# Layer 1's bias rows on their way through DRAM: one small store and a DRAM-to-DRAM copy in place of a store of 128 copies

## The chip, the cores and the metric

One Trainium2 chip, one of its cores in use. Times are device microseconds (us) of one execution of the whole program; lower is better.

## The reference: what is computed

Two decoder layers on 256 tokens of width 1024, all in float32. Layer 0 mixes tokens by a gated delta rule (8 heads), layer 1 by sparse attention (8 heads in 2 groups: compressed, selected and window branches). Both layers attend to 256 memory tokens with 4 heads, multiply by an output projection and end in a gated channel mixer.

```python
for i in range(DEPTH):                       # 2 layers
    h = rms_norm(x, norm_mix_w[i])
    mem_n = rms_norm(mem, mem_norm_w[i])
    proj = h @ w_in[i]                       # heads of the mixer, and queries for the memory
    mix = gdn_mixer(...) if i == 0 else nsa_mixer(..., rel_bias, ...)
    mo = memory_attention(qm, mem_n, mem_w_kv[i])
    x = x + concatenate([mix, mo], -1) @ w_out[i]
    x = x + conv_glu(rms_norm(x, norm_ffn_w[i]), ...)
return rms_norm(x, final_norm_w)
# in nsa_mixer, to the scores of each query t and key p:
#   bias = rel_bias[t5_bucket(t - p), head]   (32 buckets x 8 heads)
```

The change is about that last bias alone. It depends on the distance t - p only, so a head has 384 different values over the distances of two 128-token halves (some masked).

## The kernel before, in words

**How the work runs.** The program is recorded as tile operations; a list scheduler (`Sched`, with cost estimates of its own) fixes an order for each engine before the program is built, and each engine then runs its own list strictly in that order. All DMAs are issued from one list, that of SP. An SP entry whose semaphores are not up holds back all entries behind it. Every operation is issued at one line, L379 (`Op.run`), so the profile's line numbers don't tell operations apart; tile names do.

**Weights.** `Weights.prep` loads 8 blocks of 128x128 (512 KB) into a tile `wr`, ScalarE (ACT) casts it to `wh`, VectorE (DVE) subtracts to get `wl`; TensorE (PE) then does three matmuls per block (`pj<-xh,wh`, `xl,wh`, `xh,wl`). There are three buffers each of `wr`, `wh` and `wl`. For the memory's keys and values the same is done with 256 KB tiles `mr`, `mh`, `ml` and PSUM tiles `pf`.

**The place of the change** is the seam between the last memory attention of layer 0 and its output projection `w_out` (12 weight tiles of 8 blocks each). By priority the scheduler has pulled two things forward into this seam: layer 1's memory keys and values (`mr`, `pf`, `vm`) and layer 1's bias tables. The bias tables are made so: a 33x8 by 33x384 matmul gives the 384 values of each head on 8 partitions, ACT copies them to `bb` (8 partitions x 384), and one DMA writes `bb` 128 times over to the DRAM tile `sk` (8 x 128 x 384, 1.5 MB). For each head a DMA then reads `sk` with a row step of 383 in place of 384, so that partition p gets the row shifted by p: the tile `bias` (128 x 2 x 128).

```python
sk = sc.tile("sk", [H, P, HOTN], F32, "sk", 1)                       # L1171
SY.dma_start(sk, bb[:, None, :].to_broadcast([H, P, HOTN]))          # L1172
for h in range(H):                                                   # L1173
    bt = K("bias", H, shape=(P, 2, P))
    SY.dma_start(bt, sk.raw(... ap=[[HOTN - 1, P], [P, 2], [1, P]]))
```

The eight `bias` tiles are read some 280 us later, by the attention of layer 1.

Of the kernel before, what the change touches and what calls it, by code (L numbers as in the profile page):

```python
# [10 lines left out]
F32 = mybir.dt.float32  # L11
# [8 lines left out]
P = 128  # L20
# [5 lines left out]
H = 8  # L26
# [25 lines left out]
HOTN = 384  # L52
# [1 line left out]


class Sched:
    """Records tile operations, orders them with a list scheduler over the engines, then issues them."""

    ENG = ("tensor", "vector", "scalar", "gpsimd", "sync")
    LAT = {"tensor": 0.27, "vector": 0.17, "scalar": 0.2, "gpsimd": 0.18, "sync": 0.13}  # L60
# [188 lines left out]
        return out  # L249

    def sooner(self, op, e, eng_t, ready):
        """Whether engine e would finish op before the other engine that can run it."""
        f = {}
        for x, c in op.alt.items():
            t = max(eng_t[x], op.rt)
            wait = sum((o.alt[x] * 0.5 if o.alt else o.cost) for o in ready[x] if o.prio < op.prio and o.rt <= t)
            f[x] = t + wait + c
        return f[e] <= min(f.values())
# [39 lines left out]


class Sub(Vt):  # L300
    """A part of a whole-kernel tile that has its own dependences."""

    def __init__(self, base, fn, shape, tag):
        super().__init__(base.cls, shape, base.dt, tag, 1)
# [201 lines left out]
def body(ctx, tc, xT, memT, vecs, consts, rows, relb, w_few, w_in0, w_out0, w_up0, w_dn0, w_in1, w_out1, w_up1, w_dn1,  # L506
         w_mem0, w_mem1, cw1, cw2, out):
    nc = tc.nc
    pools = {}
# [9 lines left out]
    classes = dict(CLASSES)  # L519
    sc = Sched(nc, classes)  # L520
    PE, V, A, PO, SY = (sc.t[e] for e in Sched.ENG)
# [8 lines left out]
    def K(tag, bufs=2, dt=F32, shape=(P, S)):  # L530
        return sc.tile("k", shape, dt, tag, bufs)

    def Dd(tag, bufs=2, shape=(P, 512), dt=F32):
        return sc.tile("d", shape, dt, tag, bufs)

    def Sm(tag, shape, bufs=2):
        return sc.tile("s", shape, F32, tag, bufs)

    def pj(tag="pj"):
        if tag != "pj":  # L540
            return sc.tile("ps", [P, S], F32, tag, 4)
        return sc.tile("ps", [P, S], F32, "pj", 4)
# [10 lines left out]
    def mm(*a, **kw):  # L553
        PE.matmul(*a, **kw)
# [11 lines left out]
        return ps  # L566

    def proj_t(ws, b0, xs, tag="pj"):
        """Token-major products: [128 tokens, 256 columns] for both halves of the sequence."""
        ps = [pj(tag), pj(tag)]  # L570
        n = len(xs)
        for k in range(n):
            wh, wl = ws.block(b0 + 2 * k, 2)
            xh, xl = xs[k]
            for t in range(2):
                c = slice(t * P, (t + 1) * P)
                with PE.group():
                    mm(ps[t], xh[:, c], wh, start=k == 0, stop=False)
                    mm(ps[t], xh[:, c], wl, start=False, stop=False)
                    mm(ps[t], xl[:, c], wh, start=False, stop=k == n - 1)  # L580
        return ps

    def proj_few(hl, xs, n):
        """Few columns: both parts of the weights are one stationary operand of 2n columns."""
        ps = pj()
        for k in range(KD):
            xh, xl = xs[k]
            with PE.group():
                mm(ps[:2 * n], hl[:, k], xh, start=k == 0, stop=False)
                mm(ps[:2 * n], hl[:, k], xl, start=False, stop=k == KD - 1)  # L590
        return ps[:2 * n]
# [15 lines left out]
    x = [Sub(xall, lambda r, k=k: r[:, k], [P, S], f"x{k}") for k in range(KD)]  # L607
# [61 lines left out]
    def evac(ps, rs, dst):  # L669
        V.tensor_tensor(out=dst, in0=ps, in1=rs, op=OP.mult)  # L670

# [1 line left out]
    kTm, vm = {}, {}  # L673
    def mem_load(k):
        mt = Dd("mt", 4)
# [58 lines left out]
            mm(po[:, :S], vm[layer, h // 2, m2][:, (h % 2) * P:(h % 2 + 1) * P], pT[:, m2 * S:(m2 + 1) * S], start=m2 == 0, stop=m2 == 1)  # L734
        return hilo(po[:, :S], "mix", 12)

# [1 line left out]
    def ffn(layer, w_up, w_dn, rs, xs):  # L738
        wu = Weights(sc, w_up, 2 * KF * KD, "w", 3)
        wd = Weights(sc, w_dn, KD * KF, "w", 3)  # L740
# [32 lines left out]
    def normed(col, keep="row"):  # L773
        hs, acc = [], None
        for k in range(KD):
            hs.append(split(x[k], col + k, "x", KD))
            acc = sq_acc(acc, x[k])
        r = rstd_fin(acc, keep=keep)
        return (hs,) + (r if keep == "col" else (r,))

    # ================= layer 0 =================
    def x_load(k):
        SY.dma_start(xall[:, k:k + 2], xT[:, k * S:(k + 2) * S].rearrange("p (k t) -> p k t", k=2), also_out=x[k:k + 2])

# [38 lines left out]
        hs.append((hi, lo))  # L823
    mix = [None] * 12

    # decay and write strength, token-major [128, tile, head]
    ps = proj_few(wba, hs, 16)
    ba = K("ba", 1, shape=(32, S))
    A.copy(ba, ps)
# [71 lines left out]
    US = NB * (IB * P + IB)  # L901

    def silu(dst, y, src, fast):
        """silu(y), or twice that from the table that Exp is in."""
        if fast:
            A.activation(dst, src, AF.Silu)
            return
        th = K("ct")
        A.activation(th, src, AF.Tanh, scale=0.5)
        V.scalar_tensor_tensor(dst, th, 1.0, y, op0=OP.add, op1=OP.mult)  # L910
# [24 lines left out]
    def gdn_pair(p):  # L935
# [53 lines left out]
                V.scalar_tensor_tensor(AT[e][:, t], pgm[:, t * S + P:(t + 1) * S], rr[:, t:t + 1], g1[:, t], op0=OP.mult, op1=OP.mult)  # L989

        yield
        # inverses of the 16 x 16 diagonal blocks, one block on each partition
        sl = sc.tile("scl", [4 * US], F32, "scl", 2)
        for e in range(2):
            SY.dma_start(sl.raw(lambda r, e=e: bass.AP(tensor=r.tensor, offset=r.offset + 2 * e * US,
                                                      ap=[[P, P], [US, 2], [1, P]]), [P, 2, P]), LL[e])
        Lb = K("Lb", 1, shape=(4 * NB, IB, IB))
        SY.dma_start(Lb, sl.raw(lambda r: bass.AP(tensor=r.tensor, offset=r.offset,
                                                 ap=[[IB * P + IB, 4 * NB], [P, IB], [1, IB]]), [4 * NB, IB, IB]))
# [4 lines left out]
        for k in range(IB - 1):  # L1004
# [8 lines left out]
                                             ap=[[IB * IB, 4 * NB], [4 * NB * IB * IB, 2], [1, IB * IB]]),  # L1013
# [9 lines left out]
                EV.tensor_tensor(out=DX[e][:, w].rearrange("p u (c i) -> p u c i", c=NB),  # L1023
                                         in0=cd[:, w, 2 * e:2 * e + 2][:, :, None, :].to_broadcast([P, 2, NB, IB]), in1=bd, op=OP.mult)

        # doubling of the diagonal blocks: 16 to 32 over whole chunks, then by blocks of 32 and of 64
        for e in range(2):
            lm = K("lm", 4, shape=(P, 2, P))
            EV.tensor_tensor(out=lm, in0=LL[e], in1=cst[:, C_LVL - C_TRI:C_LVL - C_TRI + P][:, None, :].to_broadcast([P, 2, P]),
                             op=OP.mult)  # L1030
# [7 lines left out]
            with PE.group():  # L1038
                for t in range(2):
# [3 lines left out]
                                                      ap=[list(r.ap[0]), [S + IB, 2], [2 * IB, NB], [1, IB]]), [P, 2, NB, IB])  # L1043
# [25 lines left out]
                            V.tensor_tensor(out=DX[e][O, 0, :, E], in0=DX[e][O, 0, :, E], in1=two(p2[O, :2 * n]), op=OP.subtract)  # L1069

        yield
        # chunk recurrence and outputs
        zs = {}
        for e, h in enumerate(hd):
            ps = proj(w0, (h * 4 + 3) * KD, hs)
# [2 lines left out]
        for e, h in enumerate(hd):  # L1078
# [38 lines left out]
            y = K("oz", 1)  # L1117
# [32 lines left out]
    hs, rs = normed(V_NFFN)  # L1150
    ffn(0, w_up0, w_dn0, rs, hs)

    # ================= layer 1 =================
    hs, rs, rc = normed(V_NMIX + KD, "col")
    rcs = Sm("rcs", [P, 2], 1)
    V.tensor_scalar(rcs, rc, SCALE, None, op0=OP.mult)

    # relative-position bias tiles
    rbe = Sm("rbe", [33, H], 1)
    V.memset(rbe, NEG)  # L1160
    SY.dma_start(rbe[:32], relb)
# [2 lines left out]
    bias = []  # L1164
# [3 lines left out]
    mm(pb[:H, :HOTN], rbe, hot, start=True, stop=True)  # L1168
    bb = Dd("bb", 1, (H, HOTN))
    A.copy(bb, pb[:H, :HOTN])  # L1170
    sk = sc.tile("sk", [H, P, HOTN], F32, "sk", 1)  # L1171
    SY.dma_start(sk, bb[:, None, :].to_broadcast([H, P, HOTN]))  # L1172
    for h in range(H):  # L1173
        bt = K("bias", H, shape=(P, 2, P))
        SY.dma_start(bt, sk.raw(lambda r, h=h: bass.AP(tensor=r.tensor, offset=r.offset + h * P * HOTN + P - 1,
                                                      ap=[[HOTN - 1, P], [P, 2], [1, P]]), [P, 2, P]))
        bias.append(bt)

    w1 = Weights(sc, w_in1, 24 * KD, "w", 3)
    # keys of a group: first half of the sequence (selected, window) and compressed; second half  # L1180
    KC = 2 * P + 16
    KA = [[Dd("KF" + "hl"[i], 2, (P, KC), F32R) for i in range(2)] for g in range(G)]
    KS = [[K("KS" + "hl"[i], 2, F32R) for i in range(2)] for g in range(G)]
# [1 line left out]
    for t in pw:  # L1185
        PO.memset(t.bitcast(F32), 0.0)
    vtok = {}
    # windows of the keys and values to compress, both parts of both: one stationary operand of 120 columns
    NW = 2 * G * NCMP
    win = [Dd("win", 8, (P, 4, 2 * NW), F32R) for i in range(8)]  # L1190
    for j in range(2):
        for g in range(G):
# [9 lines left out]
            for i in range(8):  # L1202
# [3 lines left out]
                                op=OP.subtract)  # L1206
# [30 lines left out]
    for j in range(2):  # L1237
        pc = mx()
        mm(pc[:, :2 * NCMP], hid[:, j * P:(j + 1) * P], fw[:, 2 * NCMP * j:2 * NCMP * (j + 1)], start=True, stop=True)
        cc = Sm("cc", [P, 2 * NCMP])  # L1240
        A.copy(cc, pc[:, :2 * NCMP])
        ct = Sm("cth", [P, 2 * NCMP])
        A.activation(ct, cc, AF.Tanh, scale=0.5)
        w2 = K("cw2", 2, shape=(P, P))
        SY.dma_start(w2, cw2[:, j * P:(j + 1) * P])
        pc2 = mx()
        V.scalar_tensor_tensor(cc, ct, 1.0, cc, op0=OP.add, op1=OP.mult)
        if j == 0:
            mm(pc2[:, :2 * NCMP], w2, cc, start=True, stop=True)
            for g2 in range(G):  # L1250
                o, src = slice(2 * P, 2 * P + NCMP), pc2[:, g2 * NCMP:(g2 + 1) * NCMP]
                kh, kl = KA[g2]
                for t in (kh, kl):
                    V.memset(t[:, 2 * P + NCMP:].bitcast(F32), 0.0)
                A.mul(kh[:, o], src, 0.5)
                V.scalar_tensor_tensor(kl[:, o], src, 0.5, kh[:, o].bitcast(F32), op0=OP.mult, op1=OP.subtract)
        else:
            # three copies of the values on rows 0, 32, 64, for the three products of the parts
            c3 = K("c3", 1, shape=(P, G, 3, 32))
            V.memset(c3, 0.0)  # L1260
            A.copy(c3[:, :, :, :NCMP], cc.rearrange("p (g c) -> p g c", g=G)[:, :, None, :].to_broadcast([P, G, 3, NCMP]))
            for g2 in range(G):
                mm(pc2[:96, g2 * P:(g2 + 1) * P], c3[:, g2].rearrange("p a c -> p (a c)"), w2, start=True, stop=True)
            vc = K("vc", 1, F32R, (96, G, P))
            A.mul(vc, two(pc2[:96, :S]), 0.5)
            V.scalar_tensor_tensor(vc[64:], two(pc2[64:96, :S]), 0.5, vc[64:].bitcast(F32), op0=OP.mult, op1=OP.subtract)
# [218 lines left out]
```

## Time and profile before

| | |
|---|---|
| three timed runs | 844.47, 844.68, 845.36 us |
| median | 844.68 us |
| profiled execution, span of its instructions | 845.3 us |
| PE busy | 803.3 us (95%) |
| DVE / ACT / POOL busy | 603.8 / 479.6 / 169.7 us |
| mean granted clock of PE | 0.983 |
| DMA | 137.53 MB, 163 GB/s on average |

The profiled execution's own time is its span; the page tells of nothing outside it. The span lies within 0.1% of the median and inside the three runs' spread, so durations from the profile may be set against the median. A PE that is busy for 95% of the span leaves 42 us in which it is not; the rows below tell where a large part of them lies.

### The profile page before, as it was taken

The page shows a single profiled execution, that of the slowest core. Times are in us where ns is not written, and L with a number is a line of the kernel's source. Part 1 is how long each engine was busy: PE and PEld are TensorE (multiplying, and loading weights), DVE is VectorE, ACT ScalarE, POOL GpSimd, SP SyncE. Part 2 cuts the span into 40 slices and gives each one's busy share as a digit, 9 for nine tenths or more (in the row PEclk, how much of TensorE's full clock was granted, in tenths as well). Part 3 has the DMA queues.
Part 4 walks back from the last instruction along what each step waited for, and adds up shares of the span by engine and source line. Part 5 has one row for each costly group of instructions (what it writes and reads, how often), then busy time and mean ns, then how long its engine had stood idle before and what let it go on. Part 6 is the DMA issues. An engine that isn't in the chain of part 4 may idle for free.

```text
span 845.3 us, 17098 instructions
## 1 busy us (share of the span) xinstructions
PE 803.3 (95%) x6645; PEld 787.7 (93%) x6645; DVE 603.8 (71%) x1243; ACT 479.6 (57%) x995; POOL 169.7 (20%) x273
## 2 busy tenths in 40 slices
PE   6999899999964999999999999999999999999996
PEld 5999899999964999999999999999999999999996
DVE  6999888978604856776766668688687776776552
ACT  6577575667513455655544446599954655555340
POOL 2258553643101111111110130000010211111000
PEclk9999999999995999999999999999999999999998
DMA  8664346334347646665666557722255566666641
GB/s 307 209 236 141 118 115 196 104 100 120 96 64 198 206 125 187 187 192 171 180 200 181 176 166 227 230 79 85 88 175 164 188 176 196 180 196 176 181 144 50
DMA packets 53797, 137.53 MB, mean 163 GB/s; under 512 B 11555, under 2 KB 18772, under 8 KB 53716
## 3 DMA queue, kind: packets, MB, share of 16 engines
q1 hardware_dynamic: 53716, 136.44, 54.4%
q8 instruction: 52, 0.85, 0.4%
q14 instruction: 29, 0.24, 0.1%
HBM read 132.48 MB, written 3.94 MB: 161 GB/s over the span
## 4 chain that ended last, share of the span: by engine, by line
PE 73%; DMA 8%; DVE 7%; POOL 5%; issue 5%; ACT 1%; SPq 0%; POOLq 0%; ACTq 0%; DVEq 0%
PE pj L379 60%; PE mx L379 9%; DMA mr<-in_w_mem 4%; PE pf L379 3%; DVE wl L379 2%; POOL DD L379 1%; POOL tm L379 1%; DMA cd<-scd 1%; POOL sqa L379 1%; DVE DD L379 1%; DVE win L379 1%; DMA wr<-in_w_in 1%; DVE cy L379 1%; DMA ident<-in_consts 1%; ACT wh L379 1%
## 5 line engine op out<-in xcount | busy, mean ns | idle before, releaser
L379 PE MATMUL pj<-xh,wh 128*128 128x256 f32 x1152 | 333.4, 289 | 0.0
L379 PE MATMUL pj<-xh,wl 128*128 128x256 f32 x1152 | 326.4, 283 | 1.1 <-DVE wl L379 1.1
L379 PE MATMUL pj<-xl,wh 128*128 128x256 f32 x1152 | 326.2, 283 | 0.0
L379 DVE TENSOR_TENSOR wl<-wr,wh 128x1024 fp32r<-128x1024 f32 x224 | 275.6, 1236 | 35.5 <-ACT wh L379 34.3
L379 ACT CAST wh<-wr 128x1024 fp32r<-128x1024 f32 x224 | 232.0, 1042 | 34.6 <-DVE wl L379 22.6
L379 PEld LDWEIGHTS pj<-xh,wl 128*128 128x128 f32 x1152 | 220.9, 192 | 1.4 <-DVE wl L379 1.3
L379 PEld LDWEIGHTS pj<-xh,wh 128*128 128x128 f32 x1152 | 221.1, 192 | 0.7
L379 PEld LDWEIGHTS pj<-xl,wh 128*128 128x128 f32 x1152 | 221.1, 192 | 0.2
L379 PE MATMUL pj<-gh,wl 128*128 128x256 f32 x352 | 99.8, 283 | 0.0
L379 PE MATMUL pj<-gl,wh 128*128 128x256 f32 x352 | 99.8, 283 | 0.0
L379 PE MATMUL pj<-gh,wh 128*128 128x256 f32 x352 | 99.8, 283 | 0.0
L379 POOL TENSOR_TENSOR fs<-fs,rs 128x256 f32<-128x256 f32 x44 | 39.6, 899 | 215.5 <-ACT fs L379 207.3
L379 PE MATMUL pj<-mixh,wh 128*128 128x256 f32 x192 | 56.9, 296 | 18.1 <-ACT wh L379 18.1
L379 PEld LDWEIGHTS pj<-gh,wh 128*128 128x128 f32 x352 | 67.7, 192 | 0.0
L379 PEld LDWEIGHTS pj<-gh,wl 128*128 128x128 f32 x352 | 67.7, 192 | 0.0
L379 PEld LDWEIGHTS pj<-gl,wh 128*128 128x128 f32 x352 | 67.7, 192 | 0.0
L379 PE MATMUL pj<-mixh,wl 128*128 128x256 f32 x192 | 55.6, 290 | 0.5 <-DVE wl L379 0.5
L379 PE MATMUL pj<-mixl,wh 128*128 128x256 f32 x192 | 55.6, 289 | 0.0
L379 PEld LDWEIGHTS pj<-mixh,wh 128*128 128x128 f32 x192 | 38.1, 198 | 18.4 <-ACT wh L379 18.3
L379 DVE TENSOR_TENSOR fgr<-pj,rs 128x256 f32<-128x256 f32 x44 | 18.6, 422 | 49.1 <-PE pj L379 46.0
L379 POOL TENSOR_TENSOR sq<-xall 128x256 f32<-128x256 f32 x6 | 8.1, 1354 | 224.5 <-DVE xall L379 224.5
L379 DVE SCALAR_TENSOR_TENSOR fy<-fgr,vecb,fy 128x255 f32<-128x255 f32 x88 | 42.4, 482 | 10.1 <-ACT fy L379 9.6
(314 smaller groups left out, 1397.7 us busy)
## 6 DMA issues: line engine op xcount, KB each, us to landing
wr<-in_w_up SPq DMA_DIRECT2D x88, 512.0 KB, 4.3
wr<-in_w_in SPq DMA_DIRECT2D x60, 512.0 KB, 4.5
wr<-in_w_dn SPq DMA_DIRECT2D x44, 512.0 KB, 4.2
wr<-in_w_out SPq DMA_DIRECT2D x24, 512.0 KB, 4.0
mr<-in_w_mem SPq DMA_DIRECT2D x32, 256.0 KB, 3.9
wr<-in_cw SPq DMA_DIRECT2D x8, 512.0 KB, 4.7
mt<-in_memT SPq DMA_DIRECT2D x8, 256.0 KB, 6.0
sk<-bb SPq DMA_DIRECT2D x1, 1536.0 KB
```

Source lines behind the costliest of these rows:

```text
L379: i = getattr(getattr(nc, self.eng), m)(*[fix(x) for x in a], **{k: fix(v) for k, v in kw.items()})
```

## The change

`bb` is first written to DRAM once (`skr`, 8 x 384, 12 KB). A second DMA copies these 12,288 bytes from DRAM to DRAM 128 times (`sk`, now 128 rows of all eight heads, 1.5 MB in all). The eight reads keep their form, with a row step of 8 x 384 - 1.

```diff
-    sk = sc.tile("sk", [H, P, HOTN], F32, "sk", 1)
-    SY.dma_start(sk, bb[:, None, :].to_broadcast([H, P, HOTN]))
+    classes["skr"] = 1
+    pools["skr"] = pools["dram"]
+    skr = sc.tile("skr", [H, HOTN], F32, "skr", 1)
+    SY.dma_start(skr, bb)
+
+    sk = sc.tile("sk", [P, H * HOTN], F32, "sk", 1)
+    SY.dma_start(sk, skr.raw(lambda r: bass.AP(tensor=r.tensor, offset=r.offset, ap=[[0, P], [1, H * HOTN]]), [P, H * HOTN]))
     for h in range(H):
         bt = K("bias", H, shape=(P, 2, P))
-        SY.dma_start(bt, sk.raw(lambda r, h=h: bass.AP(tensor=r.tensor, offset=r.offset + h * P * HOTN + P - 1,
-                                                      ap=[[HOTN - 1, P], [P, 2], [1, P]]), [P, 2, P]))
+        SY.dma_start(bt, sk.raw(lambda r, h=h: bass.AP(tensor=r.tensor, offset=r.offset + h * HOTN + P - 1,
+                                                      ap=[[H * HOTN - 1, P], [P, 2], [1, P]]), [P, 2, P]))
         bias.append(bt)
```

The rest of the diff removes comments. Since the scheduler plans with one DMA more, the lists of the engines change near this place too.

SP's list, from the last `mr` load ahead of the bias store to the first loads of the output projection's second half. Before:

```order
L379 DMA mr_3687<-in_w_mem 128x512
L379 DMA sk_3697<-bb_3678 1024x1x384
L379 DMA mr_3737<-in_w_mem 128x512
L379 DMA mr_3742<-in_w_mem 128x512
L379 DMA bias_3776<-sk_3697 128x256
...
L379 DMA bias_3808<-sk_3697 128x256
L379 DMA mr_3839<-in_w_mem 128x512
L379 DMA wr_3861<-in_w_out 128x1024
```

And now (the left-out rows are the other six `bias` reads, as before):

```order
L379 DMA mr_3687<-in_w_mem 128x512
L379 DMA skr_3697<-bb_3678 8x384
L379 DMA mr_3710<-in_w_mem 128x512
L379 DMA sk_3728<-skr_3697 128x3072
L379 DMA mr_3764<-in_w_mem 128x512
L379 DMA bias_3803<-sk_3728 128x256
...
L379 DMA bias_3829<-sk_3728 128x256
L379 DMA wr_3838<-in_w_out 128x1024
```

The copy `sk` stands one load behind the store `skr` that it waits for; the eight reads and, behind them, `wr_3838` are still behind the filling of `sk`. The third `mr` load has gone from this place to one 15 rows further on, behind the load `wgar`.

ACT's list in the same stretch, from the last memory weights that are cast ahead of the seam to the fourth cast of weights of the output projection. Before:

```order
L379 CAST mh_3729<-mr_3687 128x512
L379 CAST mixh_3734<-mx_3733 128x256
L379 CAST mixh_3745<-mx_3744 128x256
L379 COPY mpT_3752<-mx_3751 128x512
L379 CAST mixh_3772<-mx_3771 128x256
L379 COPY mpT_3791<-mx_3790 128x512
L379 CAST mixh_3814<-mx_3813 128x256
L379 CAST mh_3828<-mr_3737 128x512
L379 ACTIVATE vm_3644<-pf_3643,rs_900_1225 128x256
L379 ACTIVATE vm_3659<-pf_3658,rs_900_1225 128x256
L379 CAST wh_3857<-wr_3312 128x1024
L379 CAST wh_3878<-wr_3337 128x1024
```

And now:

```order
L379 CAST mh_3733<-mr_3687 128x512
L379 CAST mixh_3738<-mx_3737 128x256
L379 CAST mixh_3745<-mx_3744 128x256
L379 COPY mpT_3752<-mx_3751 128x512
L379 COPY mpT_3759<-mx_3758 128x512
L379 CAST mixh_3778<-mx_3777 128x256
L379 CAST mixh_3783<-mx_3782 128x256
L379 CAST wh_3834<-wr_3312 128x1024
L379 CAST wh_3855<-wr_3337 128x1024
L379 ACTIVATE xh_3879<-xall,vec_80 128x256
L379 CAST wh_3892<-wr_3410 128x1024
...
L379 CAST wh_3932<-wr_3838 128x1024
```

The cast of the `mr` tile that is loaded right behind the bias store no longer stands ahead of the casts `wh<-wr_3312` and so on; it has gone, with the two `vm`, behind the output projection. On PE 15 matmuls (five blocks) `pf` have gone the same way. DVE's list loses one `ml` there and has it back behind the output projection.

## Rows read from the trace of the kernel before

**Rows 1.** The page: busy time (share of the span) and number of instructions of each engine.

```profile
PE 803.3 (95%) x6645; PEld 787.7 (93%) x6645; DVE 603.8 (71%) x1243; ACT 479.6 (57%) x995; POOL 169.7 (20%) x273
```

**Rows 2.** Windows around the seam: stretch, its length, busy us (instructions) of each engine, granted clock of PE (1.00 is the upper of its two levels), mean busy share of the 16 DMA engines, GB/s.

```profile
228.00:246.00 18.00, 18.00 (x138) 17.41 (x137) 4.63 (x11) 4.58 (x10) 0.00 (x0) 1.00 0.44 61
246.00:264.00 18.00, 0.16 (x2) 0.00 (x0) 0.69 (x1) 2.12 (x4) 0.00 (x0) 0.62 0.49 80
264.00:271.00 7.00, 6.32 (x28) 6.02 (x29) 6.46 (x8) 3.40 (x6) 2.20 (x2) 0.51 0.93 289
271.00:294.00 23.00, 23.00 (x194) 23.00 (x193) 19.28 (x31) 11.28 (x15) 1.09 (x1) 1.00 0.68 212
```

**Rows 3.** PE's own rows around the gap, in order of time: start, duration, operation, [idle time before and what ended it].

```profile
245.76 0.28 PE L379 MATMUL pj<-mixl,wh 128*128 128x256 f32 x1
245.88 0.28 PE L379 MATMUL pj<-mixh,wl 128*128 128x256 f32 x1
264.22 0.58 PE L379 MATMUL pj<-mixh,wh 128*128 128x256 f32 x1 [18.06 <-ACT wh L379]
...
265.48 0.58 PE L379 MATMUL pj<-mixh,wl 128*128 128x256 f32 x1 [0.46 <-DVE wl L379]
...
270.34 0.42 PE L379 MATMUL pj<-mixh,wh 128*128 128x256 f32 x1
270.55 0.41 PE L379 MATMUL pj<-mixl,wh 128*128 128x256 f32 x1
...
271.03 0.28 PE L379 MATMUL pj<-mixl,wh 128*128 128x256 f32 x1
```

**Rows 4.** ACT's rows in the same stretch.

```profile
228.18 0.47 ACT L379 COPY bb<-mx 8x384 f32<-8x384 f32 x1 [0.74 <-PE mx L379]
...
233.19 0.37 ACT L379 CAST mixh<-mx 128x256 fp32r<-128x256 f32 x1 [0.49 <-PE mx L379]
233.68 0.59 ACT L379 COPY mpT<-mx 128x512 f32<-128x512 f32 x1
235.56 0.37 ACT L379 CAST mixh<-mx 128x256 fp32r<-128x256 f32 x1 [1.29 <-PE mx L379]
...
238.28 0.37 ACT L379 CAST mixh<-mx 128x256 fp32r<-128x256 f32 x1 [1.34 <-PE mx L379]
261.88 0.62 ACT L379 CAST mh<-mr 128x512 fp32r<-128x512 f32 x1 [23.22 <-DMA mr<-in_w_mem]
...
263.13 1.04 ACT L379 CAST wh<-wr 128x1024 fp32r<-128x1024 f32 x1
```

**Rows 5.** The chain of work that ended last, between 226 and 300 us: start, length, what.

```profile
229.57 32.28 DMA mr<-in_w_mem
```

**Rows 6.** DMA issues on SP in order of time (start, time that the issue took), and what SP's list waited for between 228 and 275 us (us in total, times, longest).

```profile
228.67 0.80 SPq L379 DMA_DIRECT2D sk<-bb  x1
229.57 7.56 SPq L379 DMA_DIRECT2D mr<-in_w_mem  x1
...
237.24 4.95 SPq L379 DMA_DIRECT2D mr<-in_w_mem  x1
...
SPq L379 <- DMA sk<-bb: 19.0, 1, 19.0
...
261.24 3.86 SPq L379 DMA_DIRECT2D bias<-sk  x8
265.23 0.35 SPq L379 DMA_DIRECT2D mr<-in_w_mem  x1
265.62 0.42 SPq L379 DMA_DIRECT2D wr<-in_w_out  x1
```

**Rows 7.** Windows inside the gap (columns as in Rows 2): what moves is the store `sk<-bb` and what is left of two loads `mr`.

```profile
246.00:252.00 6.00, 0.16 (x2) 0.00 (x0) 0.00 (x0) 0.00 (x0) 0.00 (x0) 0.86 0.44 51
252.00:258.00 6.00, 0.00 (x0) 0.00 (x0) 0.00 (x0) 0.00 (x0) 0.00 (x0) 0.50 0.44 51
```

**Rows 8.** DMA issues by name: count, KB each, median us from issue to landing.

```profile
sk<-bb SPq DMA_DIRECT2D x1, 1536.0 KB
g<-gsc SPq DMA_DIRECT2D x8, 128.0 KB, 3.4
...
Lb<-scl SPq DMA_DIRECT2D x4, 32.0 KB, 1.9
gsc<-gct SPq DMA_DIRECT2D x1, 8.0 KB, 1.4
```

**Rows 9.** SP's eight reads `g<-gsc` (every partition reads the same two rows of DRAM), and the windows in which their data moves; then the window of the four final stores `out<-fin` (128 partitions to DRAM), where nothing else moves.

```profile
46.51 3.98 SPq L379 DMA_DIRECT2D g<-gsc  x8
...
48.00:50.00 2.00, 1.97 (x18) 2.00 (x19) 1.61 (x3) 2.00 (x4) 0.42 (x1) 1.00 0.76 193
50.00:52.00 2.00, 2.00 (x19) 2.00 (x18) 2.00 (x6) 0.92 (x4) 1.87 (x4) 1.00 0.85 239
842.00:844.00 2.00, 0.00 (x0) 0.00 (x0) 0.00 (x0) 0.00 (x0) 0.00 (x0) 0.50 1.00 387
```

**Rows 10.** The tile `wr` between 226 and 300 us: durations in ns (least/median/most) of its cast and subtraction, and us from a load's issue to its landing (least/median/most).

```profile
L379 ACT CAST wh<-wr x12: 1029/1038/1051, 263.1 to 291.3; 128x1024 fp32r<-128x1024 f32 x12
L379 DVE TENSOR_TENSOR wl<-wr,wh x12: 1217/1225/1653, 264.2 to 292.5; 128x1024 fp32r<-128x1024 f32 x12
DMA to landing us min/median/max: 3.5/4.7/6.9
```

**Rows 11.** The end of the output projection, where the moved work now stands: rows of SP, then of ACT, then of PE.

```profile
292.65 0.33 SPq L379 DMA_DIRECT2D wr<-in_w_up  x1
293.02 0.43 SPq L379 DMA_DIRECT2D wgar<-in_w_few  x1
...
296.43 0.35 ACT L379 CAST wga<-wgar 128x192 fp32r<-128x192 f32 x1 [1.18 <-DMA wgar<-in_w_few]
...
293.46 0.28 PE L379 MATMUL pj<-mixh,wl 128*128 128x256 f32 x1
293.58 0.28 PE L379 MATMUL pf<-mh,memh 128*128 128x256 f32 x1
```

## Prediction, made before the changed kernel was run

> **What bounds the kernel now.** I read the busy times first: PE is busy for 803.3 of 845.3 us [rows 1], so only a stretch in which PE stands still, or runs at its lower clock, can be worth much. Windows along the span show one such stretch inside the program: from 246 to 264 us PE does 0.16 us of work in 18, and from 264 to 271 it works at a granted clock of 0.51, the lower of the two levels (1.2 instead of 2.4 GHz) [rows 2]. The bias store lies in it.
>
> Then the waits, backwards. PE's rows: the last matmul before the gap starts at 245.88; the next waits 18.06 us for ACT's cast `wh`, the third another 0.46 us for DVE's `wl`, and until shortly before 271 matmuls follow each other every 0.21 us (270.34 to 270.55) where the step at full clock is 0.12 us (245.76 to 245.88) [rows 3]. ACT's rows: its list is held for 23.22 us by the cast of one `mr` tile; the `wh` cast that PE wants stands three rows behind it, and its data landed long before [rows 4]. The chain names that load too: 32.28 us from issue to use [rows 5]. SP's rows tell why it is late: it was issued right behind `sk<-bb`, took 7.56 us to issue, the load after it another 4.95 us, and the eight `bias` reads waited 19.0 us more for `sk` to land [rows 6]. So the store was issued at 228.67 and had landed at 261.2: 32.5 us for 1.5 MB. With almost nothing else in flight it moves 51 GB/s and holds a DMA share of 0.44 [rows 7]. Everything in the rings behind it, the `mr` load first, takes its pace.
>
> **What the gap costs.** The matmul at 271.03 is the 29th after the one at 245.88 (28 start between 264 and 271 [rows 2], it is the next). At 0.12 us a step it would have started at 245.88 + 29 x 0.12 = 249.4. It is 21.7 us late: 19.2 of waiting, about 2.4 of half clock. Behind it PE is busy without a hole (23.00 of 23 us [rows 2]), so an earlier PE stays earlier.
>
> **The change, part by part.** There are two doors through which the store holds PE, and they are to be priced apart.
>
> *ACT's door.* The `mh` cast behind the store no longer stands ahead of the `wh` casts; it is behind the output projection. A late `mr` can't hold `wh` any more, however slow the copy is. The buffer that `wh_3834` takes comes free 13 blocks before PE's stopping point (39 matmuls, 4.7 us); cast and subtraction take 1.04 and 1.23 us [rows 10], so both are there in time.
>
> *SP's door.* The eight reads still wait for `sk`, and `wr_3838` stands behind them. Three weight tiles (24 blocks) are already on the chip when PE gets to its old stopping point. That point is now at 246.0 - 1.8 = 244.2, since 15 `pf` matmuls of 0.12 us were moved behind. PE then has 24 x 3 x 0.12 = 8.6 us of work, until 252.8. For the third matmul of `wr_3838`'s first block (0.24 us on) cast, subtraction and 0.1 us of handing over must be done: landed by 250.7. A load takes 4.7 us to land, at worst 6.9 [rows 10]: issued by 246.0. From the first read's issue to the first `wr` it was 261.24 to 265.62, of which 0.39 was an `mr` load now gone [rows 6]: 4.0 us. So `sk` may land at 242.0 and PE does not wait. The copy can be issued once `skr` has landed: 228.67 plus 1.4 us, the landing of the 8 KB store `gsc<-gct` [rows 8]: 230.1. The copy has **11.9 us** (9.7 with the slowest `wr` landing).
>
> *The copy's own time* is the unknown; the trace has no DRAM-to-DRAM transfer. Fixed part: 1.9 us, the landing of a 32 KB load from DRAM [rows 8]. One `mr` load of 256 KB goes ahead of it in the rings: 0.7 us at 387 GB/s. Then 1.573 MB at a rate. Upper bound 387 GB/s, the best a store to DRAM reaches [rows 9]: 4.1, in all 6.7 us. Lower bound the old store's 51 GB/s [rows 7]: 30.8, in all 33.4. Between them lie the reads `g<-gsc`, where all partitions read the same 1 KB of DRAM: 193 and 239 GB/s, 216 on average [rows 9]: 7.3, in all **9.9 us**. I take that: it is the row with the copy's peculiarity (one small source for everything), in smaller pieces than the copy has. Writing to DRAM is no limit by the 387. `sk` lands at 240.0, 2.0 us before PE would notice.
>
> Why was the store slow? With a share of 0.44 [rows 7] it either had too few engines (51/0.44 = 116 GB/s on all of them: the copy 13.6, in all 16.2 us) or too few source partitions, which the copy does not have. The Trainium skill, SBUF — State Buffer, section Door 1: The DMA port swizzle, says that a transfer's rate goes by the ports its partitions reach, and that eight partitions from 0 on reach two of 16, some 27 GB/s each. By that rule the store's limit is 54 GB/s, the trace's 51 agrees, and the copy, which touches no SBUF, is free of it; by the first reading alone the copy would be 6.3 us slower than my sum. No run here shows yet which holds.
>
> *Small terms.* The extra store of 12 KB: hidden, SP's next entry but one waits for it, nothing that PE wants. The moved `pf` blocks filled PE's time between the steps of the last memory attentions; there ACT waits for PE (0.49 to 1.34 us before each `mixh` [rows 4]), not PE for ACT, so I take 0; if every one of the five blocks leaves a hole it is 1.8 us. At the far end, `mr_4255` is now issued behind `wgar`, 0.4 us after 293.02; `wgar` was cast at 296.43 [rows 11], so the tile is cast and split by about 298.4. PE begins `pf` at 293.58 [rows 11] and reaches that tile's blocks 16 blocks (5.8 us) and one `pj` block later, at 299.7 or after: hidden, with 1.3 us to spare. The move itself is neutral: 1.8 us of PE less here, 1.8 more there.
>
> **Sum.** 845.3 - 21.7 = **823.6 us** against the profiled span; against the median, 0.6 us lower, it would be 823.0. I forecast 823.5.
>
> **The rivals.**
> - *The gain in part, by SP's door.* The copy runs at about 116 GB/s or a little less: 16.2 us, `sk` lands at 246.3, 4.3 us too late, and PE waits that long behind 24 blocks. In the old gap the clock fell about 4.3 us after PE stopped (a mean of 0.86 from 246 to 252 and 0.50 after [rows 7]), so up to 2.4 us of half clock may come on top: 828 to 830. For it speaks the share of 0.44, against it the `g` reads and the final stores. The Trainium skill, DMA: Bandwidth & Descriptors, section Latency and other measured facts, gives copies between HBM tensors 207 to 214 GB/s, and speaks for this rival with 97 to 103 where all rows step by a large power of two and meet on the same channels; 128 rows read at one address could be such a case. By its full rate the copy is within 0.3 us of my sum; by 103 GB/s it takes 17.9 us, and the time is about 832. The `g` reads, all at one address, did not fall so low.
> - *Slower than before.* The reads of one 12 KB row are served one after another and the copy is no faster than the store. At 51 GB/s `sk` lands at 263.5, PE waits 21.5 us and pays 2.4 of half clock: 847.5. It decides where wait and clock reach 21.7 us, at a copy of 31.2 us (55 GB/s); each further us is lost in full. Against it: [rows 9].
> - *Holes where the `pf` blocks were*: up to 1.8 us, 825.4. It is inside the forecast's own range.
>
> **How the numbers follow.** Forecast, PE waiting under 2 us in all: 0.72, with a range of its own from 822.0 to 825.5. Gain in part, 825.5 to 832: 0.19. No gain left (the copy near 30 us): 0.02. Slower: 0.07. Within 0.2% (1.7 us) a run can't be told from no change. Faster 0.91, same 0.02, slower 0.07. The range from 822.0 to 830.0 takes the forecast's range and the nearer half of the partial case: about 8 in 10.
>
> **What would show it.** In the new profile: ACT without the 23 us wait for `mr`; `sk<-skr` issued near 230.1 and SP's wait for it under 11 us; the first `bias` read by 242; PE without a wait over 1 us between 228 and 275 and no window at 0.5 clock there. Wrong would be a PE wait for `wh` near 253 with SP's list still standing at the `bias` reads (the copy's rate), or holes on PE from 231 to 238 (the moved blocks).

## The result, and the profile after

| | before | after |
|---|---|---|
| runs | 844.47, 844.68, 845.36, 846.02 us | 821.98, 824.11, 824.31, 824.36 us |
| median | 845.02 us | **824.21 us** |
| span of the profiled execution | 845.3 us | 822.5 us (its own time 824.31) |
| mean granted clock of PE | 0.983 | 0.996 |

The ratio is 0.9739, 95% interval 0.9723 to 0.9756. The forecast was 823.5 us, its own range 822.0 to 825.5.

The page of the kernel after, busy time of each engine; it answers to [rows 1]:

```profile
PE 799.3 (97%) x6645; PEld 784.5 (95%) x6645; DVE 603.2 (73%) x1243; ACT 480.1 (58%) x995; POOL 169.1 (21%) x273
```

No engine lost an instruction. PE is busy 4.0 us less, some 3.0 of them in the stretch at half clock (28 matmuls filled 6.32 us there [rows 2]; at 0.12 us each they take 3.4), and idle 18.8 us less: the work is the same, the gap is what went. Windows around the seam, after (columns as in [rows 2]):

```profile
228.00:246.00 18.00, 18.00 (x139) 17.53 (x140) 9.91 (x19) 8.42 (x15) 1.28 (x1) 1.00 0.73 218
246.00:264.00 18.00, 18.00 (x152) 18.00 (x152) 13.90 (x24) 8.55 (x11) 1.05 (x2) 1.00 0.70 219
264.00:271.00 7.00, 7.00 (x60) 7.00 (x60) 6.27 (x12) 3.52 (x6) 1.73 (x1) 1.00 0.69 202
```

From 246 to 264 us PE does 152 matmuls where it did 2, and the clock stays at the upper level throughout. DMA moves 218 GB/s from 228 to 246, where it moved 61.

SP's issues after (columns as in [rows 6]):

```profile
228.48 0.29 SPq L379 DMA_DIRECT2D skr<-bb  x1
228.86 0.33 SPq L379 DMA_DIRECT2D mr<-in_w_mem  x1
229.87 0.58 SPq L379 DMA_DIRECT2D sk<-skr  x1
230.50 0.57 SPq L379 DMA_DIRECT2D mr<-in_w_mem  x1
238.13 3.85 SPq L379 DMA_DIRECT2D bias<-sk  x8
242.03 12.28 SPq L379 DMA_DIRECT2D wr<-in_w_out  x6
```

And what SP's list waited for on the way of the bias rows:

```profile
SPq L379 <- DMA sk<-skr: 7.0, 1, 7.0
...
SPq L379 <- DMA skr<-bb: 0.6, 1, 0.6
```

The small store held SP for 0.6 us: the copy was issued at 229.87, 1.4 us behind it. SP then waited 7.0 us for the copy, and the first read of `sk` went out at 238.13, 8.3 us after the copy's issue, where the old store had taken 32.5. The `mr` load behind it took 0.57 us to issue instead of 7.56. ACT's cast of the first weight tile that stands behind the reads in SP's list (it answers to [rows 4]):

```profile
248.43 1.05 ACT L379 CAST wh<-wr 128x1024 fp32r<-128x1024 f32 x1 [3.25 <-DMA wr<-in_w_out]
```

ACT still waits here, 3.25 us, but PE does not. The chain after, one piece of it (answers to [rows 5]):

```profile
236.27 33.83 PE pj L379 x282
```

The output projection runs as one piece of 282 matmuls, 0.12 us each. Where the gap stood in the chain of before, there is nothing but PE.

### The profile page after: what moved, and what is told of

Its sections match the earlier page's. It is cut to its first block, busy times and chain, and to the rows that moved or that the text cites. A ratio compares the mean times of both kernels' runs of the same rounds, so it can differ in the third digit from the quotient of the medians.

```text
span 822.5 us, 17100 instructions
## 1 busy us (share of the span) xinstructions
PE 799.3 (97%) x6645; PEld 784.5 (95%) x6645; DVE 603.2 (73%) x1243; ACT 480.1 (58%) x995; POOL 169.1 (21%) x273
## 4 chain that ended last, share of the span: by engine, by line
PE 84%; DVE 5%; POOL 5%; DMA 3%; issue 2%; ACT 0%; SPq 0%; POOLq 0%; DVEq 0%
PE pj L379 69%; PE mx L379 11%; PE pf L379 4%; POOL DD L379 1%; DVE wl L379 1%; DMA cd<-scd 1%; POOL tm L379 1%; POOL sqa L379 1%; DVE DD L379 1%; DVE win L379 1%; DMA ident<-in_consts 1%; DMA scd<-DD 1%; DMA Lb<-scl 0%; POOL rs L379 0%; DVE cy L379 0%
## 5 line engine op out<-in xcount | busy, mean ns | idle before, releaser
L379 PE MATMUL pj<-xh,wh 128*128 128x256 f32 x1152 | 333.0, 289 | 0.0
L379 PE MATMUL pj<-xh,wl 128*128 128x256 f32 x1152 | 325.9, 283 | 1.1 <-DVE wl L379 1.1
L379 PE MATMUL pj<-xl,wh 128*128 128x256 f32 x1152 | 325.7, 283 | 0.0
L379 DVE TENSOR_TENSOR wl<-wr,wh 128x1024 fp32r<-128x1024 f32 x224 | 275.4, 1235 | 41.2 <-ACT wh L379 39.5
L379 ACT CAST wh<-wr 128x1024 fp32r<-128x1024 f32 x224 | 232.3, 1042 | 37.4 <-DVE wl L379 24.0
L379 PEld LDWEIGHTS pj<-xh,wl 128*128 128x128 f32 x1152 | 220.5, 191 | 1.5 <-DVE wl L379 1.3
L379 PEld LDWEIGHTS pj<-xh,wh 128*128 128x128 f32 x1152 | 220.7, 192 | 0.7
L379 PEld LDWEIGHTS pj<-xl,wh 128*128 128x128 f32 x1152 | 220.8, 192 | 0.2
L379 PE MATMUL pj<-gh,wh 128*128 128x256 f32 x352 | 99.6, 283 | 0.0
L379 PE MATMUL pj<-gl,wh 128*128 128x256 f32 x352 | 99.6, 283 | 0.0
L379 PE MATMUL pj<-gh,wl 128*128 128x256 f32 x352 | 99.6, 283 | 0.0
L379 POOL TENSOR_TENSOR fs<-fs,rs 128x256 f32<-128x256 f32 x44 | 39.2, 892 | 217.2 <-ACT fs L379 209.0
L379 PEld LDWEIGHTS pj<-gh,wh 128*128 128x128 f32 x352 | 67.6, 192 | 0.0
L379 PEld LDWEIGHTS pj<-gl,wh 128*128 128x128 f32 x352 | 67.6, 192 | 0.0
L379 PEld LDWEIGHTS pj<-gh,wl 128*128 128x128 f32 x352 | 67.6, 192 | 0.0
L379 PE MATMUL pj<-mixh,wh 128*128 128x256 f32 x192 | 55.2, 288 | 0.0
L379 PE MATMUL pj<-mixh,wl 128*128 128x256 f32 x192 | 54.3, 283 | 0.0
L379 PE MATMUL pj<-mixl,wh 128*128 128x256 f32 x192 | 54.3, 283 | 0.0
L379 DVE TENSOR_TENSOR fgr<-pj,rs 128x256 f32<-128x256 f32 x44 | 18.6, 423 | 46.2 <-PE pj L379 43.1
L379 DVE SCALAR_TENSOR_TENSOR fy<-fgr,vecb,fy 128x255 f32<-128x255 f32 x88 | 42.4, 482 | 10.8 <-ACT fy L379 10.3
L379 POOL TENSOR_TENSOR sq<-xall 128x256 f32<-128x256 f32 x6 | 9.0, 1506 | 200.6 <-DVE xall L379 200.6
L379 ACT ACTIVATE fs<-fy 128x256 f32<-128x256 f32 x44 | 18.4, 418 | 54.1 <-DVE fy L379 53.6
```

The source lines that it names most:

```text
L379: i = getattr(getattr(nc, self.eng), m)(*[fix(x) for x in a], **{k: fix(v) for k, v in kw.items()})
```

## The experiments

Seven edits, and the changed kernel once more beside three of them. In the edits a transfer is exchanged after the scheduler has fixed the lists (a function `late`, called there), so that the lists of all engines stay those of the kernel named. The two lines that this takes make L381 of the line that was L379. The diffs below are cut to the lines that matter; `...` marks what is left out. The theories: the old store was slow, its pace held both doors, and the new transfer opens them (**rate**); or the gain comes from the new lists, in which `mh` stands behind the projection (**order**). Within "rate": too few source partitions, or too few engines.

### The new lists with the old store

```diff
+    def late():
+        dst = sk.raw(lambda r: bass.AP(tensor=r.tensor, offset=r.offset, ap=[[HOTN, H], [H * HOTN, P], [1, HOTN]]), [H, P, HOTN])
+        cp.calls = [("dma_start", (dst, bb[:, None, :].to_broadcast([H, P, HOTN])), {})]
...
```

> The changed kernel's lists on every engine, but sk is filled as before: one DMA that stores bb 128 times from 8 partitions (the 12 KB store skr is still issued, nothing reads it). Two-door theory: ACT is not held any more, SP is. The store goes out near 229.3 us, takes its 32 us and lands near 261.5; the bias reads and the first load of w_out behind them wait for it, PE stops near 252.5 after its 24 blocks and stands for about 21 us, then 2.4 us of half clock: span 844 to 848, no gain at all. Rival (the reordering of ACT's list made the gain): PE does not stop for long, span 823 to 828.

Measured: median 846.45 us, ratio 1.001 (0.9998 to 1.0022). SP's issues:

```profile
228.50 0.33 SPq L381 DMA_DIRECT2D sk<-bb  x1
228.87 8.81 SPq L381 DMA_DIRECT2D mr<-in_w_mem  x1
260.61 3.84 SPq L381 DMA_DIRECT2D bias<-sk  x8
```

What PE waited for from 220 to 300 us:

```profile
PE pj L381 <- ACT wh L381: 19.0, 1, 19.0
PE pj L381 <- DVE wl L381: 0.5, 1, 0.5
```

Windows (PE's busy time is the first after the length, its clock the third number from the end):

```profile
246.00:252.00 6.00, 6.00 (x51) 5.87 (x49) 0.00 (x0) 0.00 (x0) 0.39 (x1) 1.00 0.45 54
252.00:258.00 6.00, 0.08 (x1) 0.00 (x0) 0.00 (x0) 0.00 (x0) 0.00 (x0) 0.78 0.44 51
```

ACT's door is open and PE works on to 252 us, as the prediction had it ("24 blocks, until 252.8"). Then it stops for as long as before: the store lands at 260.6, and now it is SP's door that holds `wr`. The gap moved 6 us to the right and is about as long (19.5 us of waiting, where about 21 were expected). The new order by itself is worth nothing. The store went into the new layout of `sk` and took 32.1 us, so the layout it writes to is not what made it slow either.

### The old lists with the new transfers

```diff
-    SY.dma_start(sk, bb[:, None, :].to_broadcast([H, P, HOTN]))
+    cp = SY.dma_start(sk, bb[:, None, :].to_broadcast([H, P, HOTN]))
...
+    def late():
...
+        cp.calls = [("dma_start", (skr.ap(), bb.ap()), {}), ("dma_start", (dst, src), {})]
...
```

The eight reads take the new row step.

> The lists of the kernel before on every engine, with the mh cast ahead of the wh casts, but at the place of the old store SP issues the 12 KB store and, behind it, the DRAM-to-DRAM copy. Two-door theory: the copy lands near 239, the mr load behind it too, so the mh cast is done near 240 and wh is cast when its buffer comes free, PE does not stop: span 821 to 825. Rival (the reordering made the gain): ACT's list is held as before and most of the gap stays, span 835 to 845.

Measured: median 824.70 us, ratio 0.9745 (0.9722 to 0.9769). SP's issues:

```profile
230.62 0.58 SPq L381 DMA_DIRECT2D sk<-skr  x1
231.30 1.76 SPq L381 DMA_DIRECT2D mr<-in_w_mem  x2
238.83 3.85 SPq L381 DMA_DIRECT2D bias<-sk  x8
```

The whole gain, with ACT's `mh` cast still ahead of the `wh` casts: the `mr` behind the copy is no longer late, so nothing is held there. PE has no wait in this stretch. The transfer is the cause; the reordering neither adds nor takes.

### The old form of store from 8 partitions spread over 32, and over 16

A matmul with each head's column repeated 4 (or 2) times puts the eight rows on partitions 0, 4, ... 28 (or 0, 2, ... 14). The store is the old one: eight source partitions, 1024 pieces of 1536 bytes, new lists.

```diff
-    bb = Dd("bb", 1, (H, HOTN))
+    bb = Dd("bb", 1, (4 * H, HOTN))
...
+        cp.calls = [("dma_start", (dst, bb[::4][:, None, :].to_broadcast([H, P, HOTN])), {})]
```

> As the first run, with the old form of store, but bb stands on the partitions 0, 4, 8 to 28 in place of 0 to 7 (the matmul makes 32 rows, each head four times); still 8 source rows of 1536 B, 1024 pieces, 8 engines. If the close source partitions limited the store: at most half of the 387 GB/s of a store from 128 partitions, 8.1 us plus 2, sk lands near 240 and the span is 821 to 825. If the number of engines or the cost of a piece limited it: 32 us as before, DMA share 0.44, span 844 to 848.

> As the store from partitions 0, 4, 8 to 28, but from 0, 2, 4 to 14. The partitions 0 to 7 gave 51 GB/s, 0 to 28 gave 199 to 215. If the limit goes by groups of four neighbouring partitions (two groups 51, eight groups about 200), four groups give about 102 GB/s: 15.4 us and 2, sk lands near 246.7, 1.5 us later than with the copy made twice, PE waits 4 to 6 us and pays some half clock, span 828 to 831. If it only mattered that the partitions are not direct neighbours: 10 us, span 821 to 824.

Measured: spread over 32, median 825.76 us, ratio 0.9761 (0.9736 to 0.9787); over 16, 832.23 us, ratio 0.9847 (0.983 to 0.9863). SP's issues, over 32:

```profile
229.32 0.72 SPq L381 DMA_DIRECT2D sk<-bb  x1
230.09 3.32 SPq L381 DMA_DIRECT2D mr<-in_w_mem  x1
239.57 3.87 SPq L381 DMA_DIRECT2D bias<-sk  x8
```

A window of it in which little but the store moves:

```profile
237.00:239.00 2.00, 2.00 (x19) 2.00 (x18) 1.23 (x1) 0.71 (x2) 0.00 (x0) 1.00 0.53 199
```

SP's issues, over 16:

```profile
229.21 0.72 SPq L381 DMA_DIRECT2D sk<-bb  x1
229.99 5.73 SPq L381 DMA_DIRECT2D mr<-in_w_mem  x1
247.58 3.87 SPq L381 DMA_DIRECT2D bias<-sk  x8
```

Such a window of it:

```profile
239.00:241.00 2.00, 2.00 (x19) 2.00 (x19) 1.52 (x2) 0.45 (x1) 0.00 (x0) 1.00 0.45 96
```

What PE waited for there from 220 to 300 us, and then a window in which it works again (its granted clock is the third number from the end):

```profile
PE pj L381 <- ACT wh L381: 5.5, 1, 5.5
PE pj L381 <- DVE wl L381: 0.5, 1, 0.5
```

```profile
258.00:264.00 6.00, 5.54 (x31) 5.25 (x32) 5.67 (x10) 2.87 (x5) 0.00 (x0) 0.63 0.56 178
```

The same store, of the same pieces and number of source partitions, moves 51 GB/s from partitions 0 to 7 [rows 7], 96 from every second and 199 from every fourth one. Its time falls from 32.5 to 18.4 and 10.2 us. What changes is where the eight partitions lie. Counted in groups of four neighbouring partitions, two, four and eight groups are read; groups of eight (one, two, four) would fit the three rates as well, and no run here tells the two sizes apart. So it is not "too few source partitions" by their number, but their neighbourhood; and it was not too few engines, since the DMA share goes from 0.44 to 0.53 only while the rate grows fourfold. Divided by the share, as the prediction did to get 116 GB/s, the rates over 16 and over 32 give 213 and 375; the store from 128 partitions below gives 372 (398 at a share of 1.07). So over 32 a busy engine moves as much as it does there, and as far as the share can tell the partitions hold it up no more. PE's 6.0 us of waiting over 16 is SP's door again.

The Trainium skill, SBUF — State Buffer, section Door 1: The DMA port swizzle, puts four neighbouring partitions on one port and gives a port 27 GB/s. By it an estimate of the three stores' limits is 54, 109 and 218 GB/s; the trace agrees, with 51, 96 and 199.

### A store from all 128 partitions

```diff
-    bb = Dd("bb", 1, (H, HOTN))
+    bb = Dd("bb", 1, (P, HOTN))
...
+        cp.calls = [("dma_start", (dst, bb[:, None, :].to_broadcast([P, H, HOTN])), {})]
```

> The changed kernel's lists, but the matmul puts each head's row on 16 of 128 partitions and one store writes every partition's row 8 times into sk; no read of DRAM ahead of it. 1.573 MB at up to 387 GB/s: 4.1 us and about 2, sk lands near 236, two us earlier than by the copy. By the two-door theory PE notices nothing of it: span as the changed kernel within 1 us. Rival (time still hangs on when sk lands): 1 to 2 us less.

Measured: median 825.12 us, ratio 0.9764 (0.9744 to 0.9783). SP's issues:

```profile
229.07 0.42 SPq L381 DMA_DIRECT2D sk<-bb  x1
...
237.04 3.85 SPq L381 DMA_DIRECT2D bias<-sk  x8
```

One window of the store, an `mr` load beside it:

```profile
233.00:235.00 2.00, 2.00 (x16) 1.92 (x15) 0.42 (x1) 1.25 (x3) 0.00 (x0) 1.00 1.07 398
```

Data moves at 398 GB/s, and yet the store took 8.0 us to the first read, some 2 more than expected (the run does not separate its fixed part from the `mr` load). Counted from the first store's issue (`skr<-bb`, here at 228.30), the reads go out 0.9 us earlier than in the changed kernel. The time is the same: there is no wait left that a faster store could shorten.

### Two copies in a row

The copy goes to a second DRAM tile first, and from there, now with 128 different source rows, to `sk`.

```diff
+        cp.calls = [("dma_start", (s1.ap(), src), {}), ("dma_start", (sk.ap(), s1.ap()), {})]
```

> The changed kernel with the copy made twice in a row: the 12 KB row into a second DRAM tile of 1.5 MB, then that tile into sk (so the second copy reads distinct addresses), and the bias reads wait for the second. Theory: SP's door has 2.0 us to spare in the changed kernel. The second copy takes 6 to 8 us, sk lands at 244 to 246, PE waits 4 to 6 us for wh near 252.5 and may pay up to 2.4 us of half clock: span 826 to 831. Rival (the transfer is hidden now, whatever it takes): span as the changed kernel, 822 to 823. A second copy clearly faster than the first would say that reading one row 128 times costs something.

Measured: median 829.35 us, ratio 0.9812 (0.9783 to 0.9841). SP's issues:

```profile
228.39 0.33 SPq L381 DMA_DIRECT2D mr<-in_w_mem  x1
229.39 0.58 SPq L381 DMA_DIRECT2D s1x<-skr  x1
238.47 0.47 SPq L381 DMA_DIRECT2D sk<-s1x  x1
...
245.22 4.43 SPq L381 DMA_DIRECT2D bias<-sk  x8
```

What PE waited for from 220 to 300 us:

```profile
PE pj L381 <- ACT wh L381: 2.6, 1, 2.6
PE pj L381 <- DVE wl L381: 0.8, 1, 0.8
```

The first copy took 9.1 us, with an `mr` load ahead of it; the second, from distinct rows, 6.75 us. At the prediction's 0.7 us for that load, reading one row 128 times costs some 1.6 us. That is a hint, not a measurement of its own: the load's share was not varied, and the first copy's time varies by 1.3 us between two profiles of the changed kernel (below). For PE, the two copies together came 3.4 us too late, a little less than the 4 to 6 expected.

### No copy at all

The eight reads take `skr` directly, with a row step of 1, and 1.5 MB are not moved. The kernel leaves out the right shift: the bias rows come out shifted the wrong way.

```diff
+        cp.calls = []
...
+            src = skr.raw(lambda r, h=h: bass.AP(tensor=r.tensor, offset=r.offset + h * HOTN, ap=[[1, P], [P, 2], [1, P]]), [P, 2, P])
```

> The changed kernel's lists without the 1.5 MB: sk is not filled, and the eight bias reads take their rows straight from the 12 KB store with a row step of 1 (so the bias is shifted the wrong way: this part of the computation is changed). What the copy still costs in the changed kernel, its traffic included. Theory: nothing, span as the changed kernel within 1 us. Rival (the copy's 8 us of DMA still delay loads that PE waits for): 1 to 3 us less.

Measured: median 825.04 us, ratio 0.9755 (0.974 to 0.9769). SP's issues:

```profile
229.48 4.51 SPq L381 DMA_DIRECT2D bias<-skr  x8
234.04 17.78 SPq L381 DMA_DIRECT2D wr<-in_w_out  x6
```

`wr` goes out 8 us earlier than in the changed kernel, and nothing is won. What is left of the copy is fully hidden.

### The changed kernel again

> The changed kernel itself, on the chip of the three runs that follow, to compare them with: span 821 to 824.

Measured: median 824.82 us, ratio 0.9753 (0.9738 to 0.9769). SP's issues:

```profile
229.93 0.58 SPq L379 DMA_DIRECT2D sk<-skr  x1
...
239.50 3.85 SPq L379 DMA_DIRECT2D bias<-sk  x8
```

The copy took 9.6 us here, 1.3 more than in the first profile, with no effect on PE. The four kernels without a wait on PE beside it (old lists, spread over 32, 128 partitions, no copy) have medians of 824.7 to 825.8: one time, within what a measurement can tell. Their profiles say it more sharply. From the first store's issue (`skr<-bb`) to the first `pf` behind the output projection, the stretch in which the gap lay, the changed kernel takes 41.46 us in both profiles (228.48 to 269.94, 228.55 to 270.01); spread over 32, 128 partitions and no copy take 41.45 to 41.47 (228.05 to 269.52, 228.30 to 269.75, 228.09 to 269.56), and the old lists 41.44 (229.24 to 272.48) once the 1.8 us of their 15 `pf` matmuls ahead are taken off.

## Why the prediction was right, step by step

**The gap's cost, 21.7 us: right.** The first `pf` matmul behind the output projection is a landmark. Before it started at 293.58 [rows 11]; after:

```profile
269.94 0.28 PE L379 MATMUL pf<-mh,memh 128*128 128x256 f32 x1
```

That is 23.6 us earlier, of which 1.8 are the 15 `pf` matmuls that now stand behind: 21.8 us. Of these, 0.2 were there before the seam (the first store was issued at 228.48, not 228.67); the seam itself gave 21.65.

**SP's door and its deadline: right, and the runs give it as a line.** The prediction let `sk` land at 242.0, that is 13.3 us after the first store's issue (228.67). Five runs of the new lists, from the fences above and PE's waits in them (the first stores, `skr<-bb`, were issued at 228.00, 227.94 and 227.73 us in the last three). The last column is the whole stretch, first store to first `pf`; of the last three, that `pf` is:

```profile
274.68 0.28 PE L381 MATMUL pf<-mh,memh 128*128 128x256 f32 x1
277.65 0.28 PE L381 MATMUL pf<-mh,memh 128*128 128x256 f32 x1
291.03 0.28 PE L381 MATMUL pf<-mh,memh 128*128 128x256 f32 x1
```

| run | first store to first read of `sk`, us | less 13.3 | PE waited, us | first store to first `pf`, us |
|---|---|---|---|---|
| after | 9.65 | -3.7 | 0 | 41.46 |
| changed, again | 10.95 | -2.4 | 0 | 41.46 |
| two copies | 17.2 | 3.9 | 3.4 | 46.68 |
| 8 spread over 16 | 19.6 | 6.3 | 6.0 | 49.71 |
| new lists, old store | 32.9 | 19.6 | 19.5 | 63.30 |

Past the deadline each us of the transfer is about a us on PE, as the rival with the partial gain had it. The lower clock comes on top: the stretch is longer by 5.2, 8.3 and 21.8 us than in the changed kernel, 1.8 to 2.3 more than PE waited; over 16 the granted clock has a mean of 0.63 from 258 to 264 us, when PE works again. That rival put its price at 828 to 830 for a copy of 16.2 us, and about 832 at 17.9; the store of 18.4 us gave 832.23. The price was right, its condition didn't come about.

**ACT's door: right but idle.** It is open in the new lists, and would have stayed open for a slow copy. With the old lists and a fast copy it isn't needed. In the changed kernel the buffer was free earlier than the "13 blocks before PE's stopping point (39 matmuls, 4.7 us)" of the prediction: ACT cast the first of the three tiles at 236.58 without a wait for PE, 7.4 us ahead of that point (244.0 in this profile), which changes nothing. The prediction priced both doors apart, and had it taken the moved cast for the gain, it would have been wrong by all of it.

**The copy's time, 9.9 us: mis-sized by a little.** The landing of the small store, 1.4 us, was met. The copy took 8.26 us to the first read (9.57 in the second profile). With the same fixed parts of 2.6 us, 5.66 and 6.97 us are left for 1.573 MB: 278 and 226 GB/s, where the `g` reads had given 216. The windows of the copy in the kernel after, the last two numbers being DMA share and GB/s:

```profile
230.00:232.00 2.00, 2.00 (x16) 1.89 (x15) 1.43 (x3) 0.93 (x2) 0.00 (x0) 1.00 0.83 224
232.00:234.00 2.00, 2.00 (x16) 1.85 (x15) 0.86 (x3) 1.26 (x4) 0.00 (x0) 1.00 0.99 344
234.00:236.00 2.00, 2.00 (x14) 1.81 (x12) 0.15 (x1) 0.93 (x3) 0.00 (x0) 1.00 1.17 327
```

The Trainium skill, DMA: Bandwidth & Descriptors, section Latency and other measured facts, gives copies of 128 rows between HBM tensors 207 and 214 GB/s at two row pitches and 103 at pitches of 4 and 8 MiB; the 97 that the prediction counts in is for a pitch 192 bytes off, and that rows meet on the same channels is an inference of the Trainium skill, not a measurement. Here windows with 128 reads at one address ran at 327 to 344 GB/s, loads `mr` among them; nothing near 103 was seen.

**The landing of `wr`, 4.7 us: too short by 1.7.** The load issued at 242.03 was there at 248.43, after 6.4 us. Landings of `wr` from 226 to 280 us after:

```profile
DMA to landing us min/median/max: 3.3/4.8/7.8
```

The median is as before [rows 10], but this load comes behind eight reads of 128 KB, and is not a median one. Against the deadline of 250.7, which is 250.5 in this profile, it had 2.1 us to spare instead of the 3.8 that 4.7 would have left. The prediction's worst case (6.9) covered it.

**Why the store was slow: the right half of the fork.** The doubt stood in the prediction as 6.3 us of copy time; the two spread stores settle it for the source partitions, though not for their number, as the prediction's "too few" had it: the same eight were fast once they lay apart. The prediction took the copy's rate from the `g` reads and did not know which half held; the copy, which reads no SBUF, went past the store's 51 GB/s either way.

**The small terms: right.** PE is busy for the whole 18.00 us from 228 to 246, the list of its waits from 220 to 300 us is empty, and the seam gave 21.65 of the 21.7 us forecast: the moved `pf` blocks left no hole worth naming. At the far end PE goes from `pj` to `pf` without a wait.

**The sum against the median: right by two errors that cancel.** The prediction took the profiled execution's own time for its span. After, the own time lies 1.8 us above the span (824.31 to 822.5), and so it does in every run (825.32 to 823.5, 845.57 to 843.8). By these 1.8 us the profiled execution before took about 847.1 us, an estimate, 2.1 above its median and not 0.6: the frame was off by about as much. The span on its part fell by 22.8 us, not 21.7: 21.8 up to the end of the seam, and by landmarks 0.5 between there and layer 1's output projection and 0.5 behind the last weights. Nothing ties that last us to the change. The first half lies within what the profiles of the new lists differ by there (320.7 to 321.5 us for the same stretch, which took 321.0 after and, with the 15 `pf` matmuls added, 321.5 before). The second is a step ahead of the last instruction on the chain, in which no engine waits for anything shown: 1.94 us in six of the ten profiles, 2.44 or 2.45 in the other four, the kernel before and the changed kernel's second profile (span 823.5) among them. What moves it the runs don't tell. The medians differ by 20.8, and the interval of the ratio holds 21.7.

## What to carry to other kernels

Where a window shows a low rate at a steady DMA share, with one transfer in flight, ask on which partitions its SBUF side lies before asking about its size or its engines. When a slow transfer holds an engine, follow every list that stands behind it: taking the waiting instruction out of one list (ACT's) moved the gap by 6 us and saved nothing, since the next list (SP's) held the same work. And work out the transfer's deadline, since it tells where getting faster stops to pay: here 13.3 us from the first store's issue, and 8.7, 9.7 or 11.5 were the same.

## What was not expected of the hardware

- The DMA share says little of a transfer's rate. Stores from eight partitions held 0.44, 0.45 and 0.53 at 51, 96 and 199 GB/s; so an engine counts as busy here while it moves little.
- A small change of source partitions, in one matmul's width and a step of four, brought the old store to 825.76 us, where the changed kernel had 824.21 and 824.82, with no DRAM-to-DRAM copy at all.
- The copy's best window reached 344 GB/s, an `mr` load in it, against 387 for stores from 128 partitions [rows 9], though the copy both reads and writes DRAM.
- A slow transfer slows the sequencer that issues: one `mr` load took 8.81 us to issue behind the store at 51 GB/s (new lists), 5.73 behind the one at 96, 3.32 behind the one at 199, and 0.57 behind the copy.
